# Attention scores of an encoder trunk as three passes over split fp32r operands in place of one plain fp32 product

## The chip, the cores and the metric

The kernel runs on one core of one Trainium2 chip. The metric is the device time of one launch in microseconds, as the median of the runs shown. TensorE multiplies matrices, VectorE and ScalarE work elementwise, GpSimd is a fourth engine for such work, and SyncE's queue starts the transfers from HBM.

## The reference

Two layers over 512 tokens of width 1024. Each layer is a half-step SwiGLU block, a mixing block, and another half-step SwiGLU block. The mixing block projects the normalised input once and gives the columns to three mixers: RWKV-7 (4 heads, both directions), latent attention (8 heads) and retention (4 heads). Only the attention's scores are touched here:

```python
q_nope, q_pe = q[..., :64], rotary(q[..., 64:], positions)
k_nope, v = kv[..., :64], kv[..., 64:]
k_pe = rotary(kpe, positions)            # one rotary key for all heads
s = einsum('bqhd,bkhd->bhqk', qn, k_nope) + einsum('bqhr,bkr->bhqk', qp, k_pe)
p = softmax(s * 96 ** -0.5)
o = einsum('bhqk,bkhd->bqhd', p, v)
```

## The kernel before

Everything is kept as features on partitions by 512 tokens. A dense product (`mm3`, L213, and `mm3y`, L617, which also yields its cost) is made of three TensorE passes: weights and activations are each split into a part rounded to fp32r (`hi`) and the rest (`lo`), and hi x hi, hi x lo and lo x hi are accumulated. `split` (L162) makes the parts: ScalarE copies to fp32r (L164), VectorE subtracts (L165). `split2` (L598) does the same into two new tiles. Small products (the RWKV-7 recurrence, the transposes, the scores) are plain fp32.

The SwiGLU blocks (`ffn`, L462) are dense products with weights streamed in, 512 KB at a time. In `mixer` (L565) two generators are interleaved: `rwkv` (L733) yields how much dense work it wants ahead of its next step, and `dense` (L627) yields the nanoseconds of TensorE work that it has issued, so that the yields set the program's order. `dense` runs the input projection, then weaves `retention` (L1168) and `mla` (L1277), then the output projection (`woutb`, L684 to L692). The tile framework then orders each engine's instructions by priority, dependences and free tiles; an engine runs its own queue in order.

Tiles of 128x512 fp32 all come from one pool of 53 (`slot`, L142, NSLOT L30). The accumulators are in three pools of banks: `pm` (2, for dense products and scores), `pr` (4, for RWKV-7) and `pa` (2).

In `mla`, L1281 to L1285 make the rotary key `kr` for both partition halves (a product with a constant, copied by ScalarE). For each of four head pairs, `prep(n)` (L1301) projects keys and queries. A key tile `K` of 128x512 takes one half from the projection (ScalarE, L1309) and the other from `kr` (VectorE, L1310); a query tile `q` takes one half scaled by ScalarE (L1317) and the other scaled and rotated by VectorE (L1318). `scores` (L1322) makes for each of two heads and two query blocks one product of 128x128 by 128x512 (L1328), the maximum (VectorE, L1330), the exponential with its sum (ScalarE, L1333), the reciprocal (L1335) and the scaling (L1337 or L1339), and yields 858. `attend` (L1344) transposes the probabilities (L1351, copied at L1353) and multiplies by the values (L1364).

Of the kernel before, what the change touches and what calls it, by code (L numbers as in the profile page):

```python
# [10 lines left out]
F32 = mybir.dt.float32  # L11
F32R = mybir.dt.float32r
# [5 lines left out]
P = 128  # L18
# [94 lines left out]
class Kern:  # L113
# [513 lines left out]
    def dense(self, l, z, sh, mixed, g2, nxt):  # L627
# [51 lines left out]
        while t < 3000:  # L679
            st = next(mla)  # L680
            t += st
            yield st
        yield from self.weave(ret, mla, 1)
        for m in range(KD - TM):  # L684
            if m:
# [591 lines left out]
    def mla(self, l, z, mixed, ms):  # L1277
        nc = self.nc
        ckv = z["ckvn"]
        t = z["kpe"]  # L1280
        nc.vector.tensor_tensor(t, t, self.tkp, op=ALU.mult)  # L1281
        pk = self.psum(self.pa, "pkr")
        nc.tensor.matmul(pk, lhsT=self.c("krep"), rhs=t, start=True, stop=True)
        kr = self.slot("kr")
        nc.scalar.copy(kr, pk)  # L1285
        yield 858
        vh, vl = self.weights(self.ap["uv"][l], 1024)
        V = []
        for tb in range(4):
            ps = self.psum(self.pm, "pv")  # L1290
            ts_ = slice(tb * P, (tb + 1) * P)
            yield from self.mm3y(ps, [ckv[i][0][:, ts_] for i in range(2)], [ckv[i][1][:, ts_] for i in range(2)],
                                 [(vh[:, i * 512:i * 512 + 512], vl[:, i * 512:i * 512 + 512]) for i in range(2)])
            s = self.slot("V")
            nc.scalar.copy(s, ps)
            V.append(s)
        cq = [self.split2(z[f"cq{j}"]) for j in range(3)]
        qscale = 96.0 ** -0.5
        halves = (slice(0, 64), slice(64, 128))

        def prep(n):  # L1301
            wh, wl = self.weights(self.ap["uqk"][l, n], 1024)
            ps = self.psum(self.pm, "pk")
            yield from self.mm3y(ps, self.cols(wh, 2, 768), self.cols(wl, 2, 768), ckv)
            K, Q = [], []
            for hh in range(2):
                s = self.slot("K")
                a, b = halves if hh == 0 else halves[::-1]
                nc.scalar.copy(s[a, :], ps[a, :])  # L1309
                nc.vector.tensor_copy(s[b, :], kr[b, :])  # L1310
                K.append(s)
            for hh in range(2):
                ps = self.psum(self.pm, "pq")
                yield from self.mm3y(ps, self.cols(wh, 3, hh * 384), self.cols(wl, 3, hh * 384), cq)
                q = self.slot("q")
                a, b = halves if hh == 0 else halves[::-1]
                nc.scalar.mul(q[a, :], ps[a, :], qscale)  # L1317
                nc.vector.scalar_tensor_tensor(q[b, :], ps[b, :], qscale, self.tkp[b, :], op0=ALU.mult, op1=ALU.mult)  # L1318
                Q.append(q)
            state.append((K, Q))  # L1320

        def scores(n, qh):  # L1322
            K, Q = state[n]
            pes = []
            for hh in range(2):
                for qb in (2 * qh, 2 * qh + 1):
                    ps = self.psum(self.pm, "psc")
                    nc.tensor.matmul(ps, lhsT=Q[hh][:, qb * P:(qb + 1) * P], rhs=K[hh], start=True, stop=True)  # L1328
                    nm = self.small(1, "nmax")
                    nc.vector.tensor_reduce(nm, ps, axis=AX.X, op=ALU.max, negate=True)  # L1330
                    pe = self.slot("pe")
                    sm = self.small(1, "sume")
                    nc.scalar.activation(pe, ps, AF.Exp, bias=nm, accum_out=sm)  # L1333
                    ri = self.small(1, "rinv")
                    nc.vector.reciprocal(ri, sm)  # L1335
                    if len(pes) < 2:
                        nc.vector.tensor_scalar(pe, pe, ri, None, op0=ALU.mult)  # L1337
                    else:
                        nc.scalar.mul(pe, pe, ri)  # L1339
                    pes.append(pe)  # L1340
                    yield 858
            pend.append((n, qh, pes))

        def attend(n, qh, pes, pools):  # L1344
            po = self.psum(self.pa, "pmo")
            pts = []

            def flip(kb):
                pp = self.psum(pools[kb % 2], "ppt")
                for i in range(4):  # L1350
                    nc.tensor.transpose(pp[:, i * P:(i + 1) * P], pes[i][:, kb * P:(kb + 1) * P], self.c("ident"))  # L1351
                pts.append(self.slot("PT"))
                nc.scalar.copy(pts[kb], pp)  # L1353

            flip(0)
            yield 4 * 107
            for kb in range(4):
                if kb < 3:
                    flip(kb + 1)
                    yield 4 * 107  # L1360
                pt = pts[kb]
                for hh in range(2):
                    h = 2 * n + hh
                    nc.tensor.matmul(po[hh * 64:hh * 64 + 64, 0:256], lhsT=V[kb][:, h * 64:h * 64 + 64],  # L1364
                                     rhs=pt[:, hh * 256:hh * 256 + 256], start=kb == 0, stop=kb == 3)
                yield 454
            nc.scalar.copy(mixed[2 + n][:, qh * 256:qh * 256 + 256], po[:, 0:256])

        state, pend = [], []
        for n in range(4):  # L1370
            yield from prep(n)
            mixed[2 + n] = self.slot("mo")
            for qh in range(2):
                yield from scores(n, qh)
                if len(pend) > 1:
                    yield from attend(*pend.pop(0), (self.pa, self.pa))
        ms.extend(self.split2(mixed[i]) for i in (6, 7, 2, 3, 4))
        hi, lo = self.weights(self.ap["woutb"][l, 0], 768)
        self.po0 = self.psum(self.pm, "po")
        last = attend(*pend.pop(0), (self.pa, self.pm))  # L1380
        o0 = self.mm3y(self.po0, self.cols(hi, 6), self.cols(lo, 6), ms, n=6)
        for _ in range(5):
            a, b = next(last, 0), next(o0)
            yield a + b
        yield from last
        ms.append(self.split2(mixed[5]))
        yield from o0
# [121 lines left out]
```

## Time and profile before

| what | us |
|---|---|
| median of 3 runs | 2333.05 |
| lowest, highest run | 2330.82, 2336.97 |
| span of the profiled execution | 2329.9 |
| TensorE busy in it (97%) | 2269.9 |
| VectorE busy (56%) | 1299.0 |
| ScalarE busy (40%) | 932.1 |
| GpSimd busy (1%) | 32.2 |

The profile shows one execution, instruction by instruction; its own time is its span, 2329.9 us, with the launch around it in the runs' times. Starts and durations are as the profiler records them. A matmul's end is modelled with the latency of the pipeline in it, so consecutive matmuls overlap in the rows, and the distance from one start to the next is the time that the engine is held. A plain fp32 product shows as two matmul instructions, an fp32r one as a single one.

### The profile page before, as it was taken

How to read it: one execution, taken by the hardware profiler on the slowest of the kernel's cores; microseconds unless marked ns; L12 is line 12 of the kernel's file. 1: busy time of each engine (PE TensorE's matmuls, PEld its weight loads, DVE VectorE, ACT ScalarE, POOL GpSimd, SP SyncE). 2: the span in 40 equal slices, each digit the busy share in tenths (PEclk: the TensorE clock that was granted, in tenths of full speed). 3: DMA queues.
4: the chain of work that ended last, by engine and by line, in shares of the span. 5: the costliest groups of instructions: out<-in, count | busy, mean ns of one | idle time of the engine just before them, and what ended most of it. 6: DMA issues, size and time to landing. Idle time of an engine off the chain costs nothing.

```text
span 2329.9 us, 33848 instructions
## 1 busy us (share of the span) xinstructions
PE 2269.9 (97%) x14006; PEld 1804.1 (77%) x14006; DVE 1299.0 (56%) x2113; ACT 932.1 (40%) x1473; POOL 32.2 (1%) x48
## 2 busy tenths in 40 slices
PE   6999999999999999999999999999999999999998
PEld 5888888677655788888888888887776568888887
DVE  7656865469555754333455655445785566333334
ACT  3322344533656533223433223454445564322232
POOL 0000000200000000000000000011000000000000
PEclk9999999999999999999999999999999999999999
DMA  7555553212100343332435665322220012223322
GB/s 294 195 204 189 189 200 105 73 55 73 36 18 8 125 153 138 108 100 91 144 110 195 214 219 193 115 73 73 63 57 24 10 35 89 84 90 107 97 89 86
DMA packets 83770, 263.45 MB, mean 113 GB/s; under 512 B 10272, under 2 KB 13600, under 8 KB 83616
## 3 DMA queue, kind: packets, MB, share of 16 engines
q1 hardware_dynamic: 82896, 259.69, 33.7%
q8 instruction: 109, 1.79, 0.3%
q10 hardware_dynamic: 720, 1.61, 0.2%
q14 instruction: 45, 0.37, 0.0%
HBM read 257.07 MB, written 2.10 MB: 111 GB/s over the span
## 4 chain that ended last, share of the span: by engine, by line
PE 88%; DVE 6%; ACT 3%; DMA 2%; issue 1%; POOL 0%; SPq 0%; DVEq 0%; ACTq 0%
PE po L218 7%; PE po L219 7%; PE po L220 7%; PE pu L219 6%; PE pg L219 6%; PE pu L220 6%; PE pg L220 6%; PE pg L218 6%; PE pu L218 6%; PE pz L622 3%; PE pz L623 2%; PE pz L624 2%; PE psc L1328 2%; PE pmo L1364 1%; PE pgram L895 1%; PE ppt L1351 1%
## 5 line engine op out<-in xcount | busy, mean ns | idle before, releaser
L164 ACT CAST wh<-raw 128x1024 fp32r<-128x1024 f32 (+1 forms) x346 | 330.7, 956 | 986.4 <-PE pu L219 264.7
L165 DVE TENSOR_TENSOR wl<-raw,wh 128x1024 fp32r<-128x1024 f32 (+1 forms) x346 | 381.4, 1102 | 378.1 <-ACT wh L164 370.3
L218 PE MATMUL pu<-hh,wh 128*128 128x512 f32 x632 | 245.9, 389 | 0.0
L219 PE MATMUL pu<-hl,wh 128*128 128x512 f32 x632 | 245.9, 389 | 0.0
L219 PE MATMUL pg<-hl,wh 128*128 128x512 f32 x632 | 245.9, 389 | 0.0
L218 PE MATMUL pg<-hh,wh 128*128 128x512 f32 x632 | 245.9, 389 | 0.0
L220 PE MATMUL pu<-hh,wl 128*128 128x512 f32 x632 | 245.8, 389 | 0.0
L220 PE MATMUL pg<-hh,wl 128*128 128x512 f32 x632 | 245.8, 389 | 0.0
L218 PE MATMUL po<-ah,wh 128*128 128x512 f32 x616 | 239.6, 389 | 0.0
L219 PE MATMUL po<-al,wh 128*128 128x512 f32 x616 | 239.6, 389 | 0.0
L220 PE MATMUL po<-ah,wl 128*128 128x512 f32 x616 | 239.6, 389 | 0.0
L301 DVE SCALAR_TENSOR_TENSOR ada<-ada,cb 128x1024 f32<-128x1024 f32 x144 | 175.6, 1220 | 44.3 <-DMA ada<-in_wada_dram 43.9
L489 DVE TENSOR_TENSOR silu<-silu,pu 128x512 f32<-128x512 f32 x79 | 54.3, 688 | 205.1 <-PE pu L220 205.1
L219 PEld LDWEIGHTS pg<-hl,wh 128*128 128x128 f32 x632 | 118.7, 188 | 24.6
L218 PEld LDWEIGHTS pg<-hh,wh 128*128 128x128 f32 x632 | 118.6, 188 | 24.7
L218 PEld LDWEIGHTS pu<-hh,wh 128*128 128x128 f32 x632 | 118.7, 188 | 24.6
L219 PEld LDWEIGHTS pu<-hl,wh 128*128 128x128 f32 x632 | 118.6, 188 | 24.6
L220 PEld LDWEIGHTS pu<-hh,wl 128*128 128x128 f32 x632 | 118.7, 188 | 24.5
L220 PEld LDWEIGHTS pg<-hh,wl 128*128 128x128 f32 x632 | 118.7, 188 | 24.5
L218 PEld LDWEIGHTS po<-ah,wh 128*128 128x128 f32 x616 | 115.7, 188 | 24.0
L219 PEld LDWEIGHTS po<-al,wh 128*128 128x128 f32 x616 | 115.7, 188 | 24.0
L220 PEld LDWEIGHTS po<-ah,wl 128*128 128x128 f32 x616 | 115.6, 188 | 23.9
(396 smaller groups left out, 3899.3 us busy)
## 6 DMA issues: line engine op xcount, KB each, us to landing
ada<-in_wada_dram SPq DMA_DIRECT2D x144, 512.0 KB, 4.4
raw<-in_wff2i_dram SPq DMA_DIRECT2D x88, 512.0 KB, 3.5
raw<-in_wff1i_dram SPq DMA_DIRECT2D x80, 512.0 KB, 3.5
raw<-in_win_dram SPq DMA_DIRECT2D x46, 512.0 KB, 3.5
raw<-in_wff1o_dram SPq DMA_DIRECT2D x28, 384.0 KB, 3.1
raw<-in_wff2o_dram SPq DMA_DIRECT2D x28, 384.0 KB, 3.1
raw<-in_wff1o_dram SPq DMA_DIRECT2D x28, 320.0 KB, 3.0
raw<-in_wff2o_dram SPq DMA_DIRECT2D x28, 320.0 KB, 3.0
```

What stands on the lines that cost most here:

```text
L164: nc.scalar.copy(hi, src)
L165: nc.vector.tensor_tensor(lo, src, hi.bitcast(F32), op=ALU.subtract)
L218: nc.tensor.matmul(ps, lhsT=wh[i], rhs=xh, start=first and i == 0, stop=False)
L219: nc.tensor.matmul(ps, lhsT=wh[i], rhs=xl, start=False, stop=False)
L220: nc.tensor.matmul(ps, lhsT=wl[i], rhs=xh, start=False, stop=last and i == n - 1)
L301: return nc.vector.scalar_tensor_tensor(raw, raw, 1.0, box[0], op0=ALU.mult, op1=ALU.mult, accum_out=t[:, i:i + 1])
L489: nc.vector.tensor_tensor(s, s, pu, op=ALU.mult)
L622: nc.tensor.matmul(ps, lhsT=wh[i], rhs=xh, start=i == 0, stop=False)
L623: nc.tensor.matmul(ps, lhsT=wh[i], rhs=xl, start=False, stop=False)
L624: nc.tensor.matmul(ps, lhsT=wl[i], rhs=xh, start=False, stop=i == n - 1)
L895: nc.tensor.matmul(ps[s * 64:s * 64 + 64, g], lhsT=src[hs, cs], rhs=ar[hs, :, cs], start=True, stop=True)
L1328: nc.tensor.matmul(ps, lhsT=Q[hh][:, qb * P:(qb + 1) * P], rhs=K[hh], start=True, stop=True)
```

## The change

The rotary key is split once per layer into `krh` and `krl`. Each key tile becomes two, `Kh` and `Kl`: GpSimd copies the rotary half of both, and the projected half is split out of the accumulator. Each query tile is split by `split2` after it is made. A score is then three fp32r passes by `mm3` (hi x hi, hi x lo, lo x hi), and its yield is 681 in place of 858.

```diff
-        kr = self.slot("kr")
-        nc.scalar.copy(kr, pk)
+        krh, krl = self.slot("krh", F32R), self.slot("krl", F32R)
+        self.split(pk, krh, krl)
...
             for hh in range(2):
-                s = self.slot("K")
+                kh, kl = self.slot("Kh", F32R), self.slot("Kl", F32R)
                 a, b = halves if hh == 0 else halves[::-1]
-                nc.scalar.copy(s[a, :], ps[a, :])
-                nc.vector.tensor_copy(s[b, :], kr[b, :])
-                K.append(s)
+                nc.gpsimd.tensor_copy(kh[b, :], krh[b, :].bitcast(F32))
+                nc.gpsimd.tensor_copy(kl[b, :], krl[b, :].bitcast(F32))
+                self.split(ps[a, :], kh[a, :], kl[a, :])
+                K.append((kh, kl))
...
-                Q.append(q)
+                Q.append(self.split2(q))
...
-                    nc.tensor.matmul(ps, lhsT=Q[hh][:, qb * P:(qb + 1) * P], rhs=K[hh], start=True, stop=True)
+                    qs = slice(qb * P, (qb + 1) * P)
+                    self.mm3(ps, [Q[hh][0][:, qs]], [Q[hh][1][:, qs]], [K[hh]])
...
-                    yield 858
+                    yield 681
```

## Rows read from the trace of the kernel before

**Rows 1.** The page: span, TensorE's busy time, its granted clock, the last chain.

```profile
span 2329.9 us, 33848 instructions
...
PE 2269.9 (97%) x14006; PEld 1804.1 (77%) x14006; DVE 1299.0 (56%) x2113; ACT 932.1 (40%) x1473; POOL 32.2 (1%) x48
...
PEclk9999999999999999999999999999999999999999
...
PE 88%; DVE 6%; ACT 3%; DMA 2%; issue 1%; POOL 0%; SPq 0%; DVEq 0%; ACTq 0%
```

**Rows 2.** Windows: length, busy us (instructions) of PE, PEld, DVE, ACT, POOL; clock; DMA.

```profile
595.00:760.00 165.00, 161.08 (x1785) 97.75 (x1784) 92.03 (x225) 99.56 (x195) 0.00 (x0) 1.00 0.05 15
1746.00:1911.00 165.00, 161.02 (x1787) 97.47 (x1785) 92.00 (x224) 98.42 (x194) 0.00 (x0) 1.00 0.05 15
```

**Rows 3.** Waits of TensorE from 595 to 760 us: total, times, longest (us).

```profile
PE pmo L1364 <- ACT PT L1353: 1.3, 1, 1.3
...
PE psc L1328 <- DVE q L1318: 0.5, 1, 0.5
PE psc L1328 <- ACT pe L1333: 0.3, 1, 0.3
```

**Rows 4.** Groups of instructions by shape: the score product, busy us, mean ns, idle before.

```profile
L1328 PE MATMUL psc<-K,q 128*128 128x512 f32 x128 | 69.0, 631 | 1.9 <-DVE q L1318 1.1 <-ACT pe L1333 0.7
```

**Rows 5.** Timeline of TensorE, 640 to 700 us: start, duration, instruction.

```profile
644.04 0.50 PE L622 MATMUL pq<-sh,wh 128*128 128x512 f32 x1
644.38 0.39 PE L623 MATMUL pq<-sl,wh 128*128 128x512 f32 x1
644.61 0.40 PE L624 MATMUL pq<-sh,wl 128*128 128x512 f32 x1
644.93 0.68 PE L1070 MATMUL py<-NT,U 64*64 64x64 f32 x16
...
652.80 1.13 PE L1328 MATMUL psc<-K,q 128*128 128x512 f32 x2
653.85 0.33 PE L1085 MATMUL pchain<-MQ,MQ 64*64 64x64 f32 x4
```

**Rows 6.** Timelines of TensorE, 708 to 715 and 728 to 732 us.

```profile
708.19 0.48 PE L622 MATMUL pk<-sh,wh 128*128 128x512 f32 x1
...
709.66 0.38 PE L839 MATMUL ptr<-cst,ar 128*128 128x128 f32 x2
...
729.10 1.98 PE L1328 MATMUL psc<-K,q 128*128 128x512 f32 x4
731.02 0.65 PE L1364 MATMUL pmo<-PT,V 128*64 128x256 f32 x4
```

**Rows 7.** A tile split the same way, 128x512: durations in ns, least, median, most.

```profile
L164 ACT CAST sh<-mo x8: 620/621/622, 747.7 to 1910.0; 128x512 fp32r<-128x512 f32 x8
L165 DVE TENSOR_TENSOR sl<-mo,sh x8: 683/686/693, 749.1 to 1910.7; 128x512 fp32r<-128x512 f32 x8
```

**Rows 8.** VectorE's copy of the rotary key, and GpSimd's sum, as rows 7.

```profile
L1310 DVE COPY K<-kr x16: 407/422/425, 598.1 to 1867.2; 64x512 f32<-64x512 f32 x16
...
L707 POOL TENSOR_TENSOR zsum<-zc x18: 1037/1591/1597, 402.6 to 1603.7; 128x510 f32<-128x510 f32 x18
```

**Rows 9.** The query's scaling, and who waited for VectorE's part (us, times).

```profile
L1317 ACT ACTIVATE q<-pq x16: 572/592/594, 602.9 to 1872.6; 64x512 f32<-64x512 f32 x16
...
L1318 DVE SCALAR_TENSOR_TENSOR q<-pq,tkp x16: 673/686/695, 603.5 to 1873.5; 64x512 f32<-64x512 f32 x16
...
  PE psc L1328: 1.1, 2
```

**Rows 10.** Groups of the page: the split of streamed weights, busy us, mean ns.

```profile
L164 ACT CAST wh<-raw 128x1024 fp32r<-128x1024 f32 (+1 forms) x346 | 330.7, 956 | 986.4 <-PE pu L219 264.7
L165 DVE TENSOR_TENSOR wl<-raw,wh 128x1024 fp32r<-128x1024 f32 (+1 forms) x346 | 381.4, 1102 | 378.1 <-ACT wh L164 370.3
```

**Rows 11.** VectorE's blend after GpSimd's sum, as rows 7.

```profile
L709 DVE SCALAR_TENSOR_TENSOR za<-zsum,muh,za x18: 746/751/1499, 403.9 to 1605.5; 128x512 f32<-128x512 f32 x18
```

## The prediction

> **What bounds the kernel now.** I read the page first, for the engine that carries the time. The span is 2329.9 us, TensorE is busy for 97% of it at the upper of its two clock levels nearly throughout (every tenth of the clock line is 9), and the chain that ended last lies on TensorE for 88% [rows 1]. The median of the runs shown is 2333.05 us, 3.1 us above the span of the profiled execution; I make the sum in the profile's microseconds and subtract it from the median. One part in 300, 7.0 us, is about what a measurement can tell from no change.
>
> The scores lie in two stretches, one a layer, where attention and the RWKV-7 recurrence share TensorE. The windows show 161.1 of 165 us busy on TensorE there, at the upper clock (1.00), with VectorE busy for 92.0 us, ScalarE for 99.6 and GpSimd for nothing [rows 2]. So VectorE and ScalarE have about 40% to spare and TensorE has 3.9 us. The waits say the same: in 165 us TensorE waited measurably five times, the longest 1.3 us, and twice ahead of a score, 0.8 us together [rows 3]. Work taken off TensorE here should therefore come off the time, unless the stream of ready matmuls dries up.
>
> **What a score product costs.** The 64 products (2 layers, 4 head pairs, 2 halves, 2 heads, 2 query blocks) show as 128 instructions, so one plain fp32 product is a pair [rows 4]. I don't use the mean of 631 ns, which has the pipeline's tail in it, but the distance from its start to that of the next instruction. A pair that starts at 652.80 is followed at 653.85: 1.05 us. Three fp32r passes of the same shape, the query projection, start at 644.04 and are followed at 644.93: 0.89 us [rows 5]. Inside the three, the steps are 0.34, 0.23 and 0.32: a pass takes 0.23, and each border to plain fp32 work adds about 0.1. Two score pairs back to back take 1.92 us, two threesomes (708.19 to 709.66) 1.47 [rows 6], so 0.22 us is saved per product there, against 0.16 for one that stands alone.
>
> In the windows of scores most pairs stand alone, as the one of [rows 5] does, so I take a value near the lower end, 0.17: **64 x 0.17 = 10.9 us off TensorE**. The ends are 64 x 0.16 = 10.2 and 64 x 0.22 = 14.1.
>
> The Trainium skill, FP8 and Floating Point Precision, section TensorE Precision Notes, says that true fp32 takes four passes through the array. That alone would make three passes save a quarter of 4 x 0.23 = 0.92, so 0.23 a product and 14.7 us, as an estimate; the trace's borders between kinds of matmul are not in that rule, and the rows decide for 10.9.
>
> **What is added on the other engines.** Each query tile (8 a layer) is now rounded by ScalarE and then has the rounded part subtracted by VectorE. The same two instructions on another tile of 128x512 took 0.62 and 0.69 us [rows 7]. The key half that was copied by VectorE in 0.42 us goes to GpSimd, twice, and VectorE instead subtracts on the other half, 64x512 out of the accumulator, nearest to the query scaling of that shape, 0.69 us: +0.27. The rotary key adds one subtraction of 0.69. Per layer that is VectorE +8 x 0.69 + 8 x 0.27 + 0.69 = 8.4 us and ScalarE +8 x 0.62 = 5.0 us. VectorE would stand at 100 of 165 us and ScalarE at 105: no new bound. Their cover is TensorE's own queue of other work; were all of it on the path, it would be 2 x 13.4 = 26.8 us. No transfer is added, so the DMA queues and the sync queue see nothing.
>
> GpSimd gets 16 copies of 64x512 a layer. No row shows one. VectorE's copy of that shape, 0.42 us, bounds it below, and GpSimd's two-input 128x510 sum, 1.59 us at the median, above [rows 8]. Even 16 x 1.59 = 25 us fits in 165 us of an idle engine, and the rotary key is there long before the first head pair, so I put the copies themselves at nothing; were the cover gone, 1.59 us for each of 8 head pairs, 12.7 us, would lie ahead of the scores.
>
> **What becomes late.** The new instructions stand between the projection and the scores. Scaling the query takes 0.59 on ScalarE and 0.69 on VectorE now, and the score waits behind it; over both layers TensorE waited for it only 1.1 us [rows 9], against 8 x 1.28 = 10.2 us if every head pair had shown its latency. The split adds 0.62 + 0.69 = 1.31 us to it, 8 x 1.31 = 10.5 at the upper end and nothing at the lower. By the same share, 11%, it is 1.1 us; the pieces also queue on engines that are 60% busy, so I take 2.0.
>
> Behind the waiting score on TensorE's queue are transposes and RWKV matmuls placed after it; on VectorE, behind the split, are the maxima of the scores, and on ScalarE the exponentials, whose ends free the two accumulator banks for the next scores. At most the added 13.4 us a layer; TensorE's waits for such an end are 0.3 us a layer now [rows 3], so 1.0 over both layers.
>
> The low part of a query is ready last, so the third pass can be parted from the first two. Each such parting costs two borders, 0.2 us; at most 16 first scores, 3.2 us; I take a quarter, 0.8. Where TensorE waits for a bank anyway (the first scores of a layer), a shorter product wins nothing: a third of 16 products, 16 x 0.17 / 3 = 0.9.
>
> Sum: -10.9 + 2.0 + 1.0 + 0.8 + 0.9 = **-6.2 us**, so 2333.05 - 6.2 = **2326.8 us**. With the smallest deductions and the larger saving it is -14.1 (2319).
>
> **Rivals.** (1) *The gain is given back to tile slots.* All these tiles share 53 slots. Counting those alive in the code at the first query of a layer I get 49; the change needs one more for the rotary key, two for the keys and up to three while a query is split, so a tile must wait for one to come free. For it: the count. Against it: retention's tiles fall free within a few microseconds, and other matmuls stand ready. Priced at three waits a layer as long as the longest now, 1.3 us [rows 3], that is 7.8 us: 2334.6, no change.
>
> (2) *Slower: the split stands in line at every head pair.* ScalarE and VectorE run their queues in order, and weight splits of 0.96 and 1.10 us [rows 10] sit in the same queues. If each of the 8 projections meets one on both engines and TensorE has nothing else, the price is 8 x (1.31 + 0.96 + 1.10) = 27 us, and 2333.05 - 10.9 + 27 = 2349. It decides from 10.9 / 8 = 1.4 us lost per head pair, and shows as slower from 2.2. For it: the last score of a projection follows it closely already. Against it: 3.9 us of idle time in the whole stretch [rows 2].
>
> (3) *GpSimd stops VectorE.* A blend that normally took 0.75 us on VectorE took 1.50 in its longest case [rows 11], in the stage where GpSimd ran its sums. If each of the 32 new copies held VectorE for 0.75 us, that is 24 us of VectorE work; at the 11% of latency that TensorE has shown, 2.6 us and 2329.4; all of it on the path, 2351. The Trainium skill, SBUF — State Buffer, section Who interferes with whom, speaks against this change in the same way: an instruction of VectorE with two inputs in that memory and a reading one of GpSimd block each other for a whole instruction. The doubled row agrees with it.
>
> **How the numbers follow.** The saving kept, as summed, has a chance of 0.60. Its middle lies just inside the bound of 7.0 us, but each of the four deductions can be nil and the larger saving is 3.2 us more, so I give it 0.38 past the bound and 0.22 within. Rival 1 has 0.20, all within. Rival 2 has 0.14, slower. Rival 3 has 0.06, half within and half slower. So faster 0.38, no change 0.22 + 0.20 + 0.03 = 0.45, slower 0.14 + 0.03 = 0.17. Within the first case alone the range is 2319 to 2331; for eight in ten it reaches over rival 1, with what a new order of the whole stretch may cost, to 2340.
>
> **What would show it.** Right: 192 score matmuls in place of 128, threesomes 0.7 to 0.9 us from start to start, the two stretches shorter by 3 to 5 us each, TensorE's idle time in them still under 6 us, everything outside within 1 us. The split term is wrong if waits of scores for the low part of a query sum to over 5 us; rival 1 if writes of keys or queries wait for releases of slots; rival 2 if TensorE's idle time grows by over 10 us; rival 3 if VectorE's two-input instructions are twice as long beside the copies. The forecast as a whole falls if threesomes are cut into single passes, or if the order of work, worked out anew, opens gaps elsewhere in the mixer.

## The result, and the profile after

The change made the kernel slower: 2365.49 us (median of 4 runs, 2356.62 to 2366.47) beside 2334.93 (4 runs), a difference of 30.6 us and a ratio of 1.0128 with a 95% interval of 1.0102 to 1.0153. The prediction was 2326.8, its range ended at 2340. The page of the profiled execution, as [rows 1]:

```profile
span 2364.6 us, 34112 instructions
...
PE 2279.9 (96%) x14070; PEld 1829.1 (77%) x14070; DVE 1314.9 (56%) x2131; ACT 941.5 (40%) x1489; POOL 54.2 (2%) x80
...
PEclk9999999999999999999999999999999999999999
```

The page tells little: TensorE still has 96% of the span and the clock line is all nines. But TensorE is busy for 10.0 us *longer*, although its work became less. The windows of [rows 2] show why:

```profile
595.00:760.00 165.00, 151.04 (x1666) 100.53 (x1666) 87.45 (x202) 97.02 (x188) 10.65 (x16) 0.94 0.05 15
1746.00:1911.00 165.00, 151.69 (x1740) 104.06 (x1735) 97.65 (x203) 100.42 (x189) 11.43 (x16) 0.96 0.06 18
```

Two numbers moved: TensorE idles for 14.0 and 13.3 us where it idled for 3.9 and 4.0, and its granted clock is 0.94 and 0.96 where it was 1.00.

A fixed window holds different work in the two kernels, so from here on I cut by the work: from the start of the last matmul that makes attention's values (`pv`) to the first product with `wouta`, which needs the RWKV output. The windows of before, one a layer:

```profile
592.70:783.80 191.10, 187.18 (x1930) 118.84 (x1929) 109.81 (x247) 111.89 (x213) 0.00 (x0) 1.00 0.11 34
1744.10:1935.40 191.30, 187.32 (x1930) 118.84 (x1930) 109.88 (x247) 111.17 (x212) 0.00 (x0) 1.00 0.11 32
```

and of after:

```profile
595.70:801.90 206.20, 192.06 (x1963) 130.52 (x1962) 117.05 (x255) 116.72 (x220) 10.65 (x16) 0.95 0.10 30
1763.40:1969.40 206.00, 190.76 (x1963) 130.12 (x1963) 117.44 (x255) 115.70 (x219) 11.43 (x16) 0.96 0.10 30
```

I split each length into idle time (length less PE's busy time), time lost to the clock (length times what the granted clock lacks of 1.00, to about 1 us a row) and the rest, TensorE's work at the full clock (waits shorter than a matmul's modelled tail are in it). Both layers together: before 382.4 = 7.9 + 0.0 + 374.5; after 412.2 = 29.4 + 18.6 + 364.3. **The work fell by 10.2 us, idle time rose by 21.5 and the clock took 18.6**: 29.8 of the 34.7 us between the spans. The rest lies ahead of the first cut (3.0), between the layers (1.2) and at the end (0.7). The split describes one execution of each kernel, and the work term is good to some 4 us: by the same split the unchanged matmuls come to 372.3 in e4 and to 378.9 in e16 (388.7 = 9.8 + 0.0 + 378.9; both are the kernel before with another yield), where the kernel before has 374.5.

Where the idle time is, in the waits of TensorE in the first layer's stretch of scores, 617 to 750 us (total, times, longest), to be read beside [rows 3]:

```profile
PE psc L218 <- ACT pe L1335: 4.3, 8, 1.1
PE pchain L1085 <- DVE MQ L1086: 2.2, 4, 1.0
PE pq L622 <- DVE Kl L165: 1.4, 2, 1.1
PE psc L218 <- DVE q L1319: 1.1, 1, 1.1
PE pk L622 <- ACT pe L1335: 0.7, 1, 0.7
PE pbh L720 <- DVE diagh L717: 0.6, 1, 0.6
PE pyt L1122 <- DVE ar L1061: 0.6, 1, 0.6
```

Three kinds: scores and projections waiting for the exponential that frees an accumulator bank (5.0), the RWKV recurrence waiting for VectorE (`pchain`, `pyt`: 2.8), and waits for the splits' chain (`Kl`, `q`: 2.5). The groups of the score, as [rows 4], both layers:

```profile
L218 PE MATMUL psc<-Kh,sh 128*128 128x512 f32 x64 | 33.2, 519 | 11.2 <-ACT pe L1335 8.9 <-DVE q L1319 2.3
...
L220 PE MATMUL psc<-Kh,sl 128*128 128x512 f32 x64 | 29.0, 452 | 0.0
L219 PE MATMUL psc<-Kl,sh 128*128 128x512 f32 x64 | 27.8, 434 | 0.0
```

The idle time ahead of a score is 11.2 us, was 1.9. An undisturbed threesome is what [rows 5] promised: here 617.37 to 618.23, 0.86 us, where a pair took 1.05. The last two rows show one cut apart (its first pass, `L218`, starts ahead of the rows), the third pass 3.8 us after the second:

```profile
617.37 0.47 PE L218 MATMUL psc<-Kh,sh 128*128 128x512 f32 x1
617.67 0.40 PE L219 MATMUL psc<-Kl,sh 128*128 128x512 f32 x1
617.91 0.40 PE L220 MATMUL psc<-Kh,sl 128*128 128x512 f32 x1
618.23 0.39 PE L1210 MATMUL prk<-vret,kw 128*64 128x64 f32 x5
...
669.00 0.50 PE L219 MATMUL psc<-Kl,sh 128*128 128x512 f32 x1
...
672.79 0.51 PE L220 MATMUL psc<-Kh,sl 128*128 128x512 f32 x1
```

In the whole timeline 12 of the 64 threesomes are cut, in e3 (the change with the old yield, below) 4. At full clock the pieces hold the engine for 0.43 us (one pass) and 0.63 us (two), medians; together that is 1.06 us, what a pair takes, so a cut threesome saves nothing. The 29 that stand whole and alone take 0.88 us at the median.

The new instructions last about what was taken for them from [rows 7, 8] (ns, least, median, most):

```profile
L164 ACT CAST sh<-q x16: 617/620/622, 610.4 to 1900.3; 128x512 fp32r<-128x512 f32 x16
...
L165 DVE TENSOR_TENSOR Kl<-pk,Kh x16: 681/688/695, 603.5 to 1894.6; 64x512 fp32r<-64x512 f32 x16
L165 DVE TENSOR_TENSOR sl<-q,sh x16: 670/682/693, 611.0 to 1901.0; 128x512 fp32r<-128x512 f32 x16
...
L1309 POOL CAST Kh<-krh x16: 607/608/1223, 597.4 to 1881.9; 64x512 fp32r<-64x512 f32 x16
...
L1310 POOL CAST Kl<-krl x16: 603/616/1616, 598.0 to 1883.4; 64x512 fp32r<-64x512 f32 x16
```

VectorE's new subtractions don't overlap with GpSimd's copies in time. Subtractions that the kernel had already do, and they are longer than in the kernel before, where `wl` took 1.23 us at most and `sl<-zcq` 0.69:

```profile
L165 DVE TENSOR_TENSOR wl<-raw,wh x346: 812/1224/1567, 16.6 to 2329.9; 128x1024 fp32r<-128x1024 f32 x109, 128x768 fp32r<-128x768 f32 x64
...
L165 DVE TENSOR_TENSOR sl<-zcq,sh x6: 678/782/1091, 600.3 to 1768.8; 128x512 fp32r<-128x512 f32 x6
```

The `wl` of 1.57 us starts at 598.07, beside two copies on GpSimd; the `sl<-zcq` of 1.09 us at 1767.81 beside one that took 1.06. Over both layers VectorE's instructions beside the copies are about 1.6 us longer together.

GpSimd's copies also wait. Their input, the split rotary key, is there at 582. In the first layer's second head pair the projection of the keys ends at 634.6, and the first copy starts only when the last reader of another tile (`diagh`) has ended:

```profile
634.21 0.40 PE L624 MATMUL pk<-sh,wl 128*128 128x512 f32 x1
...
644.42 0.61 POOL L1309 CAST Kh<-krh 64x512 fp32r<-64x512 f32 x1 [43.75 <-PE pbh L720]
```

The other three head pairs' copies start in the same way, at the end of an instruction that neither makes nor reads the split rotary key: a wait for a tile slot, as far as the trace can tell. (In the kernel before, too, the second head pair's key was ready late, 15.4 us after its projection; here it is 16.6.)

What the new order did to the recurrence is in the timeline of TensorE about the last score of the first layer. Before, the recurrence's fourth and last unit (its first `pchain`) starts within 4 us of the last scores:

```profile
736.58 1.45 PE L1328 MATMUL psc<-K,q 128*128 128x512 f32 x3
...
740.37 0.27 PE L1085 MATMUL pchain<-MQ,MQ 64*64 64x64 f32 x2
```

After, it starts 18.5 us behind:

```profile
749.88 0.40 PE L220 MATMUL psc<-Kh,sl 128*128 128x512 f32 x1
...
768.36 0.27 PE L1085 MATMUL pchain<-MQ,MQ 64*64 64x64 f32 x2
```

From the last score to the first `wouta` product it is 46.4 us before and 52.0 after, in both layers.

### The profile page after: what moved, and what is told of

It is laid out like the page before. It is cut to its first block, busy times and chain, and to the rows that moved or that the text cites. A ratio compares the mean times of both kernels' runs of the same rounds, so it can differ in the third digit from the quotient of the medians.

```text
span 2364.6 us, 34112 instructions
## 1 busy us (share of the span) xinstructions
PE 2279.9 (96%) x14070; PEld 1829.1 (77%) x14070; DVE 1314.9 (56%) x2131; ACT 941.5 (40%) x1489; POOL 54.2 (2%) x80
## 4 chain that ended last, share of the span: by engine, by line
PE 86%; DVE 7%; ACT 3%; DMA 2%; issue 1%; POOL 0%; SPq 0%; DVEq 0%; ACTq 0%
PE po L218 7%; PE po L219 7%; PE po L220 7%; PE pu L220 6%; PE pg L220 6%; PE pg L219 6%; PE pu L219 6%; PE pg L218 6%; PE pu L218 6%; PE pz L622 3%; PE pz L623 2%; PE pz L624 2%; PE pmo L1366 2%; PE pgram L895 1%; DVE prod L937 1%; PE ppt L1353 1%
## 5 line engine op out<-in xcount | busy, mean ns | idle before, releaser
L218 PE MATMUL pu<-hh,wh 128*128 128x512 f32 x632 | 246.1, 389 | 0.0
L218 PE MATMUL pg<-hh,wh 128*128 128x512 f32 x632 | 246.1, 389 | 0.0
L218 PE MATMUL po<-ah,wh 128*128 128x512 f32 x616 | 239.9, 389 | 0.0
L218 PEld LDWEIGHTS pg<-hh,wh 128*128 128x128 f32 x632 | 118.7, 188 | 24.6
L218 PEld LDWEIGHTS pu<-hh,wh 128*128 128x128 f32 x632 | 118.7, 188 | 24.5
L218 PEld LDWEIGHTS po<-ah,wh 128*128 128x128 f32 x616 | 115.7, 188 | 24.0
```

The lines of the kernel that those rows point to most:

```text
L218: nc.tensor.matmul(ps, lhsT=wh[i], rhs=xh, start=first and i == 0, stop=False)
```

## The experiments

Each was timed beside the kernel before, whose medians were 2331.31 (e1 to e4), 2332.95 (e5 to e8), 2332.69 (e9 to e12), 2333.17 (e13 to e16) and 2333.43 (e17, e18). Ratios are to these. For the main ones I give the split of the length into idle, clock and work, made as above from one execution each.

### The yield alone

The first batch separates the three things in the change: the passes, the splits and the yield. e4 is the kernel before with nothing but the yield; e3 is the change with the yield of before.

```diff
-                    yield 858
+                    yield 681
```

> The kernel before with the yield of 681 alone. Theory A and rival C: within 4 us of before, 2330 to 2339. Rival B: 2350 to 2365.

2342.40, ratio 1.0041 (1.0013 to 1.0068): the number in the yield, which computes nothing, costs about 10 us. 389.3 = 13.1 + 3.9 + 372.3.

```profile
595.10:791.10 196.00, 189.49 (x1930) 121.67 (x1929) 110.09 (x247) 111.81 (x212) 0.00 (x0) 0.98 0.11 32
1751.70:1945.00 193.30, 186.72 (x1930) 119.90 (x1929) 110.10 (x247) 110.81 (x212) 0.00 (x0) 1.00 0.11 32
```

The same instructions, 1930 a window, with 5.2 us more idle time and a lower clock in the first layer.

> The change with the old yield of 858 in the scores. Theory A: within 5 us of the change, 2360 to 2370. Rival B: most of the loss gone, 2325 to 2340.

2340.47, ratio 1.0037 (1.0024 to 1.0049): with 858 the change regains 25 of the 31 us, but is still slower than before. 387.3 = 20.0 + 0.0 + 367.3. The cut stretches are 4.9 us longer than before's, the profiled execution 12.5 (2342.4, clock 0.992, beside 2329.9, clock 0.995).

```profile
596.10:789.80 193.70, 183.65 (x1962) 124.72 (x1961) 116.56 (x255) 116.94 (x220) 11.29 (x16) 1.00 0.10 32
1753.30:1946.90 193.60, 183.61 (x1962) 124.70 (x1961) 116.52 (x255) 115.58 (x218) 11.29 (x16) 1.00 0.10 32
```

Part of the rest stands just ahead of the cut, between the product that makes the rotary key and the last `pv`: the same 303 matmuls in before and in e3, at a lower clock in e3.

```profile
565.10:592.70 27.60, 24.07 (x303) 17.94 (x301) 24.05 (x21) 16.61 (x28) 0.00 (x0) 0.94 0.22 67
565.40:596.20 30.80, 26.75 (x303) 20.17 (x301) 24.62 (x22) 16.69 (x28) 0.00 (x0) 0.85 0.24 70
```

To see whether the time follows the yield or whether each new order is a draw, I ran further values, for the change (e7, e10, e15) and for the kernel before (e8, e16).

> The whole change with the score's yield at 1050, about what a single plain product held TensorE for in the trace of before (1.05 us). 681 gave 2365.5, 858 2340.5. Theory 'order': the smaller the yield, the more attention is put ahead of the RWKV steps, and RWKV's serial chain is left for the end; a larger yield moves RWKV ahead, and the time falls further: 2328 to 2338, with the half-clock time before the end of the mixer below the 31 us of 858. Rival '858 is the balance': attention is left over at the end instead, 2341 or more.

> The kernel before with nothing but the score's yield at 1050 in place of 858. 681 gave 2342.4, 858 2331.3. Theory 'order': it falls or stays, 2322 to 2331. Rival '858 is the balance': 2334 or more. Whatever the change gains has to be compared with this one too, since a new yield is not part of the three passes.

> The whole change with the score's yield at 780, between 681 (2365.5 us) and 858 (2340.5); 1050 gave 2357.7. Theory 'a balance of recurrence and leftover': the time is smooth in the yield with its least near 858, so 780 gives 2343 to 2355. Rival 'every order is a draw': any value is as likely to come out low; below 2338 or above 2360 would speak for it.

> The change with the score's yield at 900; 681, 780, 858 and 1050 gave 2365.5, 2355.0, 2340.5 and 2357.7. Theory 'balance, smooth with a low near 858': 2338 to 2346. Rival 'every order is a draw': outside that.

> The kernel before with its score's yield at 780; 681, 858 and 1050 gave 2342.4, about 2332.5 and 2336.0. Theory 'balance': between 2333 and 2341, and the change's loss beside it, 2355.0 less this, is larger than the 8 us at 858. Rival 'draw': outside that.

| yield | the change, us (ratio, interval) | before, us (ratio, interval) |
|---|---|---|
| 681 | 2365.49 (1.0128, 1.0102 to 1.0153) | 2342.40 (1.0041, 1.0013 to 1.0068) |
| 780 | 2354.99 (1.0091, 1.0076 to 1.0106) | 2339.37 (1.0025, 1.0015 to 1.0035) |
| 858 | 2340.47 (1.0037, 1.0024 to 1.0049) | 1 |
| 900 | 2342.03 (1.0046, 1.0029 to 1.0062) | |
| 1050 | 2357.65 (1.0103, 1.0069 to 1.0137) | 2336.03 (1.0015, 0.9999 to 1.0030) |

All values lie on two curves with their low near 858, where e10, e15 and e16 were expected if it is a balance. So it is a balance and no draw: with a small yield more attention is put ahead of each RWKV step and the recurrence falls behind; with a large one attention itself is drawn out. The kernel before shows both in its first layer. From the first score to the last it is 125.2 us with 681, 127.4 with 858 and 132.9 with 1050; from the last score to the first `wouta` product it is 52.1, 46.4 and 43.9. In all four kernels with 681 (the change, e1, e2, e4) that product comes 33.4 to 33.5 us after the recurrence's last unit has begun, against 43.4 in before, so with 681 the end waits for the recurrence's last unit. The change's curve is also the steeper one. My guess in e7 that a larger yield helps was wrong.

### The passes alone

e1 and e5 multiply one fp32r tile by another three times and split nothing, with yield 681 and 858 (the low parts are left out):

```diff
-                s = self.slot("K")
+                s = self.slot("K", F32R)
...
-                q = self.slot("q")
+                q = self.slot("q", F32R)
...
-                    nc.tensor.matmul(ps, lhsT=Q[hh][:, qb * P:(qb + 1) * P], rhs=K[hh], start=True, stop=True)
+                    qs = slice(qb * P, (qb + 1) * P)
+                    self.mm3(ps, [Q[hh][:, qs]], [Q[hh][:, qs]], [(K[hh], K[hh])])
```

> Leaves out the low parts: queries and keys are written once as fp32r, the same tile is used in all three passes, so TensorE's work and the yield of 681 are those of the change while VectorE, ScalarE, GpSimd and the count of tiles are those of before. Theory A (the splits between projection and scores starve TensorE, and starved it is granted the lower clock): faster than before by 8 to 11 us, about 2325, clock 0.995. Rival B (the new yield reorders the whole stretch for the worse): as slow as the change, about 2365. Rival C (the shorter products themselves leave TensorE idle behind the softmax and drop the clock): 2335 to 2365, with a lower clock.

2338.36, ratio 1.0027 (1.0014 to 1.0040), 4 us under e4. 389.6 = 21.0 + 5.9 + 362.7.

> The three passes without the splits (both factors are one fp32r tile, so the low parts are left out and the two extra passes multiply the same tile), and the score's yield back at 858. With yield 681 this kernel took 2338.4 us beside 2331.3 of the kernel before and 2342.4 of the kernel before with yield 681: the passes alone saved 4.0 us there. Theory 'order': the yield is the cost, the passes do save: with 858 the time is 2331.3 less 4 to 11, so 2320 to 2327. Rival 'shorter products leave TensorE idle': the saving turns into waits whatever the yield, 2330 to 2338.

2333.16, ratio 1.0002 (0.9988 to 1.0016): no gain clear of the noise. Yet the saving is there: 383.9 = 13.9 + 3.9 + 366.2, so the work fell by 8.3 us, and idle time (+6.0) and the clock (+3.9) took it back.

```profile
592.80:783.90 191.10, 183.79 (x1962) 124.95 (x1961) 109.31 (x247) 112.15 (x213) 0.00 (x0) 1.00 0.11 35
1744.40:1937.20 192.80, 186.25 (x1962) 126.50 (x1961) 109.11 (x247) 110.92 (x212) 0.00 (x0) 0.98 0.10 33
```

In the first layer the length is 191.1 us in both kernels, with 3.4 us less of TensorE's time in it: TensorE did not set that length. The score's group says what the freed time waits for:

```profile
L218 PE MATMUL psc<-K,q 128*128 128x512 f32 x64 | 31.5, 492 | 6.2 <-ACT pe L1334 4.9 <-DVE q L1318 1.2
```

4.9 us for the exponential, where [rows 4] had 0.7: the dense pool's two banks are freed at the softmax's pace, and a shorter product only waits longer for the next bank. e13 gives every second score a bank of the RWKV pool:

```diff
-                    ps = self.psum(self.pm, "psc")
+                    ps = self.psum((self.pm, self.pr)[qb % 2], "psc")
```

> The three passes without splits at yield 858 (the low parts are left out, as before), with every second score in a bank of the RWKV pool, so that scores that stand back to back don't share the two banks of the dense pool. With the dense pool alone this kernel showed 4 waits of scores for the exponential that frees a bank, 2.4 us in the first layer's stretch, and 2333.2 us in all, no gain. Theory 'banks': the waits go and 3 to 6 us of the saving appear: 2326 to 2330. Rival 'recurrence': TensorE then waits for VectorE in the recurrence instead, or RWKV misses its bank: 2331 to 2338.

2346.22, ratio 1.0063 (1.0044 to 1.0082). The waits of scores went,

```profile
L218 PE MATMUL psc<-K,q 128*128 128x512 f32 x64 | 32.0, 500 | 0.0
```

but RWKV's matmuls wait in their place (560 to 800 us):

```profile
PE pys L1097 <- DVE pys L1092: 2.7, 2, 1.4
...
PE pnt L1027 <- ACT aT L841: 1.8, 1, 1.8
```

The second wait is for ScalarE's copy, the first for a clearing of the bank that VectorE runs behind the softmax (`L1338` just ahead of it in VectorE's queue). e13 shows that the scores' waits for a bank can be had away. It does not show that the saving can be kept, nor which limit comes next: RWKV now shares its banks with the scores, so its waits may be of e13's own making. (The cut stretches of e13 hold 2027 matmuls for 1962, another piece of the order.)

### The splits alone

e2 and e6 make the change's splits but one plain product a score, of the high parts for even query blocks and of the low parts for odd ones (the cross terms are left out), with yield 681 and 858:

```diff
-                    self.mm3(ps, [Q[hh][0][:, qs]], [Q[hh][1][:, qs]], [K[hh]])
+                    pt = qb % 2
+                    nc.tensor.matmul(ps, lhsT=Q[hh][pt][:, qs].bitcast(F32), rhs=K[hh][pt].bitcast(F32), start=True, stop=True)
```

> All splits, copies on GpSimd and tiles of the change, yield 681, but one plain fp32 product per score, over the high parts for even and the low parts for odd query blocks (other values than the reference's). Theory A: slower than the change or equal, 2365 to 2378, since the cost stays and the 10.9 us saved go. Rival B: about 2365. Rival C: near before, 2335 to 2345, since the products are as long as before.

2352.93, ratio 1.0069 (1.0039 to 1.0098). 401.5 = 22.1 + 6.0 + 373.4.

> The splits of keys and queries as in the change, but one plain fp32 product a score (the two cross terms are left out: the high parts are multiplied for even query blocks, the low parts for odd ones), and the yield at 858. With yield 681 it took 2352.9 us, the kernel before with 681 2342.4, so there the splits cost 10.5 us. Theory 'order and splits add up': 2331.3 + 10.5 = 2342. Rival 'the splits hurt only in the order that 681 gives': within 3 us of 2331.3.

2342.94, ratio 1.0042 (1.0029 to 1.0055): the splits cost 10 us under either yield. 390.2 = 15.3 + 2.0 + 372.9: no work, all idle time and clock.

```profile
595.60:791.20 195.60, 187.92 (x1930) 119.03 (x1929) 117.17 (x255) 116.47 (x219) 10.79 (x16) 0.99 0.10 32
1752.20:1946.80 194.60, 186.94 (x1930) 118.33 (x1929) 117.12 (x255) 115.93 (x220) 11.40 (x16) 1.00 0.10 32
```

VectorE has 7.3 us more a layer, near the predicted 8.4, and is still free for 40% of the window. Why then do they cost? The groups of TensorE's instructions, both layers, say where:

```profile
L1367 PE MATMUL pmo<-PT,V 128*64 128x256 f32 x256 | 43.0, 405 | 4.5 <-ACT PT L1356 4.4
...
L1331 PE MATMUL psc<-Kl,sl 128*128 128x512 f32 x64 | 35.5, 636 | 3.8 <-ACT pe L1336 2.4 <-DVE q L1319 1.3
L1331 PE MATMUL psc<-Kh,sh 128*128 128x512 f32 x64 | 34.8, 625 | 1.0 <-ACT pe L1336 1.0
...
L1199 PE MATMUL prs<-zrq,zrk 64*128 64x128 f32 x64 | 10.2, 304 | 5.6 <-DVE rp L1201 5.6
```

The values' products wait for the copied probabilities for 4.4 us (2.7 before), the scores for the exponential for 3.4 (0.7), retention for VectorE's `rp` for 5.6 (0.5; 1.8 and nothing inside the cuts). Inside the cuts these three make 6.3 of the 7.4 us of added idle time. They are softmax and retention, whose instructions share ScalarE's and VectorE's queues with the splits. A score waits for its query hardly longer than before (1.3 for 1.1), and no matmul waits for `Kl`. I tried several answers to why. e12 takes two tile slots from the kernel before (`NSLOT = 51`):

> The kernel before with 51 tile slots in place of 53, to price the slots that the change needs. If tile slots bind (the prediction's first rival), taking two away costs by itself, 2337 or more; if not, 2331 to 2335.

2331.81, ratio 0.9992 (0.9980 to 1.0003): two slots fewer cost nothing to a kernel that by the prediction's count uses 49. The change needs up to 55 by that count, so this does not test rival 1; the change with more slots was not run. e14 puts the splits and the scaling ahead in the queues:

```diff
+                with self.tc.high_priority(offset=1000):
...
+                    Q.append(self.split2(q))
```

> The change with yield 858, with the scaling and the splits of keys and queries put ahead of other ready work in the engines' queues (a higher priority, as the weights' splits have). Beside 2340.5 without it. Theory 'latency ahead of the scores': 2331 to 2337. Theory 'work between the steps of the recurrence': the splits now go ahead of the recurrence's own steps, no gain, 2339 to 2350.

2340.75, ratio 1.0037 (1.0024 to 1.0050), e3's own. But the priority hardly moved the splits: from the end of a query's projection to the end of its split, summed over the 16 queries, it is 71.5 us in e3 and 70.9 here (42.0 in before, to the end of the scaling), and for the keys' 8 projections 71.1 and 69.0. So e14 doesn't tell whether serving them earlier would help. e9 leaves the scores as before and makes all the splits beside them, read by nobody:

```diff
...
                 K.append(s)
+                kh, kl = self.slot("Kh", F32R), self.slot("Kl", F32R)
...
                 Q.append(q)
+                self.split2(q)
```

> The kernel before, yield 858, with all splits of the change added beside it and read by no score: the rotary key, the projected half of each key and each query are split, GpSimd makes its 16 copies a layer, and the scores stay plain products of the unsplit tiles. The splits that scores read cost 10 us (2342.9 beside 2333.0). Theory 'work': the added instructions on VectorE and ScalarE stand between the steps of the RWKV recurrence, whoever reads their result: 2340 to 2345. Rival 'latency': what costs is that a score waits for its split; unread they cost nothing, 2331 to 2335.

2354.76, ratio 1.0089 (1.0074 to 1.0104), with 405.8 = 21.0 + 12.2 + 372.6: unread they cost even more, twice as much (this kernel also keeps the key copies that the change drops, and its cut holds 1876 matmuls for 1930, so its split of the length compares less well). So the price is paid without any score reading a split. That speaks for the added work and tiles themselves, but the subtraction still holds the key's accumulator bank, read or not: here TensorE waits for it (`pq <- DVE Kl`, 0.8 us in the first layer). e11 subtracts the queries' low parts on GpSimd, e17 splits the queries there altogether; the edit is e17's.

```diff
-                Q.append(self.split2(q))
+                qh, ql = self.slot("sh", F32R), self.slot("sl", F32R)
+                nc.gpsimd.tensor_copy(qh, q)
+                nc.gpsimd.tensor_tensor(ql, q, qh.bitcast(F32), op=ALU.subtract)
+                Q.append((qh, ql))
```

> The change with yield 858, and the low part of each query subtracted on GpSimd in place of VectorE: 8 instructions of 0.69 us a layer leave VectorE's queue, the latency ahead of a first score grows by about 1 us (the two-input sum on GpSimd took 1.59 us in the kernel before). Beside 2340.5 for the change with 858. Theory 'work on VectorE': 2331 to 2337. Rival 'latency ahead of the score': 2342 to 2348. Within 3 us of 2340.5: neither, or both.

> The change with yield 858 and the queries split wholly on GpSimd, rounding and subtraction, so that 8 x 0.62 us a layer leave ScalarE and 8 x 0.69 leave VectorE, and some 3 us of latency come ahead of each head pair's first score. Beside 2340.5. Theory 'work of the query splits on VectorE and ScalarE': 2331 to 2336. If it stays at 2338 to 2346, the cost isn't in the query splits' time on these two engines; it is then in the keys or in what the new tiles do to the order.

2344.02, ratio 1.0044 (1.0029 to 1.0059), and 2347.46, ratio 1.0069 (1.0044 to 1.0094): no relief. Both take work off VectorE but add latency (a subtraction takes 1.27 us on GpSimd for 0.68 on VectorE) and GpSimd instructions beside VectorE's, so they don't clear the work on the two engines either. e18 splits the keys only.

> The kernel before, yield 858, with the rotary key and the keys split as in the change and the queries left whole; a score is one plain product of the query with the key's high part (even query blocks) or low part (odd ones), so the cross terms are left out. Key and query splits together cost 10 us (2342.9). If the key splits carry it: 2340 or more. If the query splits do: 2331 to 2335. If each carries its share of the instructions: 2336 to 2340.

2339.39, ratio 1.0028 (1.0016 to 1.0040), 388.0 = 11.9 + 1.9 + 374.2: the keys carry some 6 of the 10 us (4 to 9 of 7 to 13 by the intervals), with 2.8 of the 7.3 us that the splits add to VectorE a layer. One candidate is the bank again: the key's accumulator was freed by one ScalarE copy and is now held until VectorE has subtracted behind it, and in the change the next projection waits for just that (`pq <- DVE Kl`, above). But in the traces of e3, e6 and e18 no matmul waits for `Kl`, and the cost is there. The waits that do grow in e18 are those of scores for the exponential (0.7 to 3.0 us over both layers). Which of the work, the copies on GpSimd or the tile slots makes the softmax late stays open.

Of the expectations, those of e2, e4, e9, e13 and e17 came out outside every range that I had given. No version here beats the kernel before; the best that computes what the change computes is e3, with e14 alike.

## Why the prediction was wrong

**The saving was right in size.** 10.9 us off TensorE, ends 10.2 to 14.1; the work in the stretches fell by 10.2 (to some 4 us), and whole threesomes took 0.86 to 0.89 us where pairs took 1.05. By the Trainium skill's rule (FP8 and Floating Point Precision, TensorE Precision Notes: four passes for true fp32) the ratio would be 0.75, as an estimate; the rows show 0.85, so the borders that I kept in were worth keeping.

**The added work was right**: VectorE +7.3 us a layer for 8.4, the durations as taken. GpSimd's copies took 0.61 us, between the bounds of 0.42 and 1.59 (the longest, 1.62, just above).

**The failed step is "What becomes late"**: deductions of 4.7 us in all, with nothing for the new yield and nothing for the clock, where TensorE's added idle time and clock were 40.1. Term by term:
- *Queueing, 1.0 us, and bank-paced first scores, 0.9, for both layers.* I scaled the wait for a bank by what the kernel before showed, 0.3 us a layer, and let only a layer's first scores be paced by it. But that wait depends on how soon the next score comes, so a shorter product lengthens it: 0.7 us before, 4.9 in e5, with neither the splits nor a new yield, 8.9 after.
- *Split latency, 2.0.* Scores waiting for the query rose from 1.1 to 2.3 us, projections waiting for `Kl` are 1.4 us in the first layer: these waits were near the term, and yet the splits cost 10 us (e6). Most of the idle time that they add is in waits for the softmax and for retention, 6.3 of 7.4 us over both layers; my queueing term meant the former and had 1.0 for it.
- *Partings, 0.8.* I took 4 cuts; there were 12, each losing the 0.18 us that a whole threesome saves, about 2 us. That is small beside the rest.
- *The yield.* I copied it from the diff and gave it no term. It is the weight by which the whole mixer is ordered; alone it costs about 11 us (e4), and within the change 25 (e3). The range and my closing sentence named a new order as what could upset the forecast, but gave it no price and no chance of its own.
- *The clock.* "At the upper level nearly throughout" was read as a property of the kernel. In the change it fell behind stretches in which TensorE had idled (last section), and in the profiled execution that took 18.6 us.

In time the parts make 11.1 (e4), 0.2 (e5) and 10.0 (e6), 21.3 of the 30.6 us. Idle time nearly adds up: +5.2 for the yield, +6.0 for the passes, +7.4 for the splits make 18.6 of the 21.5 measured. The clock does not: 3.9 + 3.9 + 2.0 = 9.8 of 18.6. So most of what the change with 681 loses beyond its parts is clock, in these executions.

**The rivals.** Rival 1 (slots) stays open. Its sign is in the trace of after: GpSimd's writes of keys start at the release of other tiles. What that costs no run prices, since e12 didn't reach the change's need. Rival 2 has its sign, TensorE's idle time grew by over 10 us, but waits for the splits themselves (`Kl`, `q`) are only 2.5 us in the first layer's stretch of scores. Whether the splits standing in line cost more than that is not shown, since e14 didn't serve them earlier. Rival 3 has a part of its sign: beside GpSimd's copies VectorE's two-input subtractions took up to 1.57 for 1.23 us and 1.09 for 0.68, and a copy up to 1.62 for 0.61. The Trainium skill (SBUF — State Buffer, Who interferes with whom) says that an instruction of VectorE with two inputs in that memory contends with one of GpSimd that reads it; these rows agree. Some 1.6 us on VectorE over both layers is far from the 24 of the rival, but it falls just ahead of the first scores for the most part.

## What to carry to other kernels

Where two streams are interleaved by estimated costs, a change of an estimate is a change of the kernel: cost it, and try the new product under the old weight first. Work taken off the busiest engine pays only while something else can fill the hole: look up what paces its next instruction (here a bank that the softmax frees) before counting the saving. Compare kernels by cutting at the same work and splitting the length into idle, clock and work; the page's busy share shows none of the three. And look into the trace of a control to see that its edit moved what it was to move: e14's didn't.

## What the runs showed of the hardware

In these traces the granted clock fell where TensorE had idled just before. Windows of after (two that follow each other, and a third at full clock):

```profile
725.00:735.00 10.00, 8.31 (x72) 5.75 (x68) 8.88 (x17) 5.21 (x9) 0.00 (x0) 1.00 0.14 39
735.00:742.00 7.00, 6.30 (x29) 3.52 (x29) 3.82 (x13) 5.00 (x11) 0.00 (x0) 0.52 0.00 0
742.00:752.00 10.00, 9.95 (x132) 6.61 (x126) 3.10 (x9) 5.46 (x14) 0.00 (x0) 1.00 0.01 2
```

Ahead of the fall TensorE was busy for 8.31 of 10 us, with a wait of 1.13 us for a query in it; then the clock stands at the lower of its two levels (1.2 GHz) for about 7 us, in which 29 matmuls pass, and is back at the upper one. So idle time is paid for twice where the clock follows it, which I had not expected of waits this short: over the cut stretches the kernel before idled for 7.9 us and lost nothing to the clock, the change idled for 29.4 and lost 18.6 more. It does not always follow: e3 idled for 20.0 us and lost nothing there, though more than before ahead of the cut (clock 0.85 beside 0.94, above). The spread of one kernel's runs goes with the clock too: the kernel before took 2327.95 us at a mean clock of 0.996 and 2341.46 at 0.992.
